# Attention: the weights for v taken from the sums' exponentials by fp32 transposes, instead of from transposed logits

## The chip, the cores and the metric

One NeuronCore of a Trainium2 chip runs the whole program; the other cores are idle. The metric is the device time of one execution in microseconds. The engines meant below are PE (TensorE: matrix products; PEld is its loading of weights), DVE (VectorE), ACT (ScalarE), POOL (GpSimd) and SP, whose queue issues the DMAs. PE's result goes to PSUM, which has room for 8 tiles of 128 x 512 fp32; DVE and ACT read it there.

## The reference

Two pre-norm residual layers over x (1 x 1024 x 1024, fp32) and a final RMSNorm. Layer 0 is a gated linear recurrence; layer 1 is attention with 16 heads of 64 and a forget gate, which is where the change lies:

```python
def fox_mixer(h, w_in, b_f, w_out):
    u = h @ w_in                                  # q, k, v, gate: 1024 each; f: 16
    ...
    cum = jnp.cumsum(jax.nn.log_sigmoid(f_logit), axis=1)
    # for each block of 128 queries:
        logits = jnp.einsum("bqhd,bkhd->bhqk", q_blk, kf) * scale
        logits = logits + (cq_blk[..., :, None] - ck[:, :, None, :])
        logits = jnp.where(mask, logits, NEG_INF)          # causal
        p = jax.nn.softmax(logits, axis=-1)
        o = jnp.einsum("bhqk,bkhd->bqhd", p, vf)
    y = o * jax.nn.silu(gate)
    return y @ w_out
```

The kernel's result has to stay close to fp32, so each product of two matrices is made of rounded halves: a value is split into hi (fp32r) and lo (the rest), and three products (hi hi, hi lo, lo hi) are added.

## The kernel before

The program has three stages. The first layer runs to about 430 us; then come its output projection, the norm and the first projections of layer 1 (to about 500 us); then the heads of attention, one after the other, to about 1120 us, with the output projection behind the last of them. This change concerns the heads.

For each head, q and k are projected for a pair of heads at a time (`kq_units`), split into hi and lo, and brought by DMA (`load`, L563) into two operand tiles: T (keys) and U (queries), 128 partitions x 2 x 1024, one of each for even and for odd heads. Their rows hold the halves and the forget gate's cumulative sums, so that two products give a logit with its gate term. A head has two halves c of 512 queries, and two functions work on each:

- `maxima(hd, c)` (L635): for each of four blocks of 128 queries, two products give the logits S with queries on partitions and keys along the row (L658, L659). DVE adds the causal mask and takes the maximum (L663); ACT takes the exponential in place and its sum (L666), of which only the sum is used. A transpose `mrow` (L672) and a product on DVE (L673) then write the negated maxima into four rows of U, so that the next function's logits come out with the maximum subtracted.
- `weigh(hd, c)` (L705): for pairs j of key blocks, two products (L727, L728) give the logits ST again, transposed: keys on partitions, queries along the row. ACT takes the exponential p (L733, L736), POOL sets the upper triangle of the diagonal block to zero (L741), DVE splits p into ph (L81, in `to_hi`) and pl (L86, in `to_lo`), and PE multiplies them with v into O (L761, L762).

An fp32r product in this stage is never narrower than 256 columns: S is widened by

```python
hi_ = max(hi_, lo_ + 256)          # L657
q0 = min(max(begin, j * P), end - 256)          # L723, ST and thereby O
```

S and ST share two PSUM slots of two banks each (tag "S"). While one half is weighed, the maxima of the next half are taken: `run(order, weigh, maxima, fill)` (L790) steps through a string, in which 0 is a step of the first function, 1 of the second, and "." a step of `fill`, the projections for later heads or, from head 13 on, the output projection (`partial`). `ORDERS` (L28) holds these strings. The framework's scheduler may then shift instructions within each engine's order by its own estimates.

Tiles of tag xp (three buffers) hold the finished heads' results y on their way back from DRAM (`load_y`, L809) and the residual stream in `partial` (L822).

## Time and profile before

| | us |
|---|---|
| median of 3 runs | 1159.39 (1158.55 to 1160.67) |
| the profiled execution | 1157.61 |
| its span (first to last instruction) | 1155.8 |
| PE busy | 1129.7 |
| DVE busy | 828.2 |
| ACT busy | 596.3 |
| POOL busy | 336.3 |

The profile is of one execution. In its rows "L727 PE MATMUL ST<-U,T" is line 727 of the kernel, on PE, a product that writes tile ST from U and T; behind the bar stand the group's busy time, the mean of one in ns, and the idle time of the engine just ahead of it, with what ended that. A fp32 product leaves two records (two passes), a transpose one. Durations of PE records overlap, since products are pipelined.

### The profile page before, as it was taken

What the parts mean: (1) busy time and instruction counts of PE and PEld (TensorE: products, weight loads), DVE (VectorE), ACT (ScalarE), POOL (GpSimd) and SP (SyncE); (2) the same over time, 40 slices, a digit from 0 to 9 for tenths busy, and PEclk for the clock granted to TensorE, in tenths of its full rate; (3) what the DMA queues carried; (4) which work ended last, traced back from release to release, by engine and by line L of the source; (5) the groups of instructions that cost most, each with busy time, mean ns of one, the idle gap of its engine ahead of it and who ended that gap; (6) DMA issues with size and microseconds to landing.
All of it is one profiled execution on the core that took longest, in us unless ns stands there. A gap on an engine that the chain in (4) does not pass through costs nothing.

```text
span 1155.8 us, 15813 instructions
## 1 busy us (share of the span) xinstructions
PE 1129.7 (98%) x5653; PEld 946.9 (82%) x5653; DVE 828.2 (72%) x1311; ACT 596.3 (52%) x1010; POOL 336.3 (29%) x328
## 2 busy tenths in 40 slices
PE   9999999999999999999999999999999999999995
PEld 7788888888888887978888988889888898777795
DVE  7589766677566889556877757777577776577776
ACT  8388345345544656454554545545455454445343
POOL 1212202112021103342333333323333334141445
PEclk9999999999999999999999999999999999999998
DMA  6111111111111124351343323433234331646544
GB/s 211 51 41 50 51 51 55 42 50 41 51 59 38 55 72 151 100 142 38 92 120 92 92 65 92 120 91 85 65 92 110 85 90 60 181 132 178 162 129 146
DMA packets 62701, 104.89 MB, mean 91 GB/s; under 512 B 8792, under 2 KB 27864, under 8 KB 62624
## 3 DMA queue, kind: packets, MB, share of 16 engines
q1 hardware_dynamic: 62624, 103.90, 32.1%
q8 instruction: 44, 0.72, 0.3%
q14 instruction: 33, 0.27, 0.1%
HBM read 62.78 MB, written 15.93 MB: 68 GB/s over the span
## 4 chain that ended last, share of the span: by engine, by line
PE 46%; DVE 6%; ACT 2%; DMA 2%; issue 1%; POOL 1%; DVEq 0%; ACTq 0%; SPq 0%; POOLq 0%
PE gps L111 6%; PE gps L113 6%; PE gps L112 6%; PE ST L727 3%; PE O L762 3%; PE S L659 2%; PE ST L728 2%; PE S L658 2%; PE O L761 2%; PE vps L523 2%; PE vps L521 2%; PE vps L522 2%; PE ops L111 2%; PE ops L113 2%; PE ops L112 2%
## 5 line engine op out<-in xcount | busy, mean ns | idle before, releaser
L86 POOL TENSOR_TENSOR wl<-wf,wh 128x512 fp32r<-128x512 f32 (+2 forms) x130 | 190.1, 1467 | 499.5 <-ACT wh L75 424.2
L111 PE MATMUL gps<-hh,wh 128*128 128x512 f32 x576 | 226.6, 394 | 0.5 <-DVE qkl L559 0.5
L113 PE MATMUL gps<-hl,wh 128*128 128x512 f32 x576 | 226.9, 394 | 0.0
L112 PE MATMUL gps<-hh,wl 128*128 128x512 f32 x576 | 226.6, 393 | 0.1
L75 ACT CAST wh<-wf 128x512 fp32r<-128x512 f32 (+2 forms) x156 | 94.0, 607 | 137.8 <-PE gps L113 43.3
L666 ACT ACTIVATE S<-S,st 128x128 f32<-128x128 f32 (+7 forms) x128 | 91.4, 714 | 114.1 <-DVE st L663 113.1
L113 PEld LDWEIGHTS gps<-hl,wh 128*128 128x128 f32 x576 | 108.3, 188 | 24.3
L112 PEld LDWEIGHTS gps<-hh,wl 128*128 128x128 f32 x576 | 108.5, 188 | 21.9 <-POOL wl L86 0.6
L111 PEld LDWEIGHTS gps<-hh,wh 128*128 128x128 f32 x576 | 108.4, 188 | 21.8 <-DVE qkl L559 0.9
L81 DVE CAST ph<-p 128x512 fp32r<-128x512 f32 (+2 forms) x130 | 80.0, 625 | 57.2 <-ACT p L733 30.1
L86 DVE TENSOR_TENSOR pl<-p,ph 128x512 fp32r<-128x512 f32 (+2 forms) x130 | 118.3, 927 | 2.4
L741 POOL TENSOR_SCALAR_AFFINE_SELECT p<-p 128x128 f32<-128x128 f32 (+1 forms) x128 | 49.1, 400 | 194.0 <-ACT p L736 95.0
L663 DVE CUSTOM_DVE_ANT_0 S<-S,mask 128x128 f32<-128x128 f32 (+7 forms) x128 | 96.6, 758 | 5.1 <-PE S L659 4.1
L355 DVE TENSOR_TENSOR x<-x,ops 128x512 f32<-128x512 f32 x80 | 54.0, 681 | 51.0 <-PE ops L113 50.9
L111 PE MATMUL ups<-hh,wh 128*128 128x512 f32 x192 | 76.1, 396 | 3.1 <-DVE us L265 1.9
L113 PE MATMUL ups<-hl,wh 128*128 128x512 f32 x192 | 76.0, 396 | 0.2
L112 PE MATMUL ups<-hh,wl 128*128 128x512 f32 x192 | 75.5, 393 | 0.0
L733 ACT ACTIVATE p<-ST 128x512 f32<-128x512 f32 (+1 forms) x68 | 53.0, 786 | 40.7 <-PE ST L728 37.6
L521 PE MATMUL vps<-wh,hh 128*128 128x256 f32 (+1 forms) x256 | 72.7, 285 | 0.0
L523 PE MATMUL vps<-wl,hh 128*128 128x256 f32 (+1 forms) x256 | 72.5, 285 | 0.2 <-POOL wl L86 0.2
L522 PE MATMUL vps<-wh,hl 128*128 128x256 f32 (+1 forms) x256 | 72.6, 284 | 0.0
L727 PE MATMUL ST<-U,T 128*128 128x512 f32 (+1 forms) x198 | 67.8, 350 | 2.3 <-ACT S L666 2.2
(192 smaller groups left out, 2580.9 us busy)
## 6 DMA issues: line engine op xcount, KB each, us to landing
wf<-in_w SPq DMA_DIRECT2D x100, 256.0 KB
wf<-in_wo SPq DMA_DIRECT2D x64, 128.0 KB
T<-qkh SPq DMA_DIRECT2D x28, 256.0 KB
U<-qkh SPq DMA_DIRECT2D x28, 256.0 KB
x<-in_xt SPq DMA_DIRECT2D x16, 256.0 KB
x1d<-x SPq DMA_DIRECT2D x16, 256.0 KB
wf<-in_wv SPq DMA_DIRECT2D x16, 256.0 KB
xp<-x1d SPq DMA_DIRECT2D x16, 256.0 KB
```

The costliest lines, as they stand in the source:

```text
L75: nc.scalar.copy(hi, src)
L81: eng.tensor_copy(hi, src)
L86: return eng.tensor_tensor(lo, src, f32(hi), ALU.subtract)
L111: nc.tensor.matmul(o, wh, xh[:, cs], start=i == 0, stop=False)
L112: nc.tensor.matmul(o, wl, xh[:, cs], start=False, stop=False)
L113: nc.tensor.matmul(o, wh, xl[:, cs], start=False, stop=i == len(pairs) - 1)
L521: nc.tensor.matmul(pt, xh, wh, start=k == 0, stop=False)
L522: nc.tensor.matmul(pt, xl, wh, start=False, stop=False)
L523: nc.tensor.matmul(pt, xh, wl, start=False, stop=k == KT - 1)
L663: nc.vector.tensor_tensor_reduce(S[:, :n], S[:, :n], mask[:, SEQ - n :], -1.0, -NEG, ALU.add, ALU.min, accum_out=m)
L666: seen[0] = nc.scalar.activation(S[:, :n], S[:, :n], AF.Exp, bias=f32(m), scale=-1.0, accum_out=sums[:, i : i + 1])
L727: nc.tensor.matmul(A[:, jj, :n], T[s][:, 0, ks], U[s][:, 0, q0:end], start=True, stop=False)
```

## The change

The exponentials that ACT takes for the sums are kept, in fp32 tiles p0 to p7 in SBUF, one for each block of 128 queries. They already have the maximum subtracted and the mask in them. `weigh` no longer computes logits: for each key block it turns the 128 x 128 blocks of p with PE transposes (fp32, against the identity) into a PSUM tile pt; ACT copies pt to ph, DVE subtracts to pl, and the products with v follow. The transposed logits, their exponentials, the selects on POOL, the maxima's transpose and the product on DVE are gone. A diagonal block now has its true width, so that the last key block of each half gives a product of 128 columns.

U is now three tiles of half the length: the first halves of even and odd heads share one (U0, tag "U"), and `load_q` loads each half by itself. The place of the copies to ph and pl in the buffers changes (three of 512 columns instead of two of 2 x 512). xp has two buffers instead of three, and the residual stream in `partial` uses two of another tag ("R"). The forget gate's scratch tiles move to other tags, and the steps in `ORDERS` are fewer, since the maxima have one step less.

```diff
-ORDERS = (("1.10111.0.10.", "1.1010.1.0.1..10"), (".1101.1..00..11.", "111.0.0.0.11.01...."))
+ORDERS = (("1.1011..0.10.", "1.1010.1.0....0"), (".1101.1..00..1.", "111.0.0.0.1.0...."))
...
-        U = [tu.tile([P, 2, SEQ], F32R, tag=f"U{s}", name=f"U{s}") for s in range(2)]
+        U0 = tu.tile([P, 2, HALF], F32R, tag="U", name="U")
+        U = [(U0, tu.tile([P, 2, HALF], F32R, tag=f"U{s}", name=f"U{s}")) for s in range(2)]
...
+        def load_q(hd, c):
+            s = hd % 2
+            u = U[s][c]
+            hi, lo = (f32(z[s * HD : (s + 1) * HD, halves[c]]) for z in kq[hd // 2, 0])
+            nc.sync.dma_start(f32(u[:64, 0]), hi)
+            nc.sync.dma_start(f32(u[64:, 0]), hi)
+            nc.sync.dma_start(f32(u[:64, 1]), lo)
+            nc.sync.dma_start(f32(u[64:66, 1]), cumd[hd, :, halves[c]])
...
+                p = ps_[i] = at.tile([P, n], F32, tag=f"p{i}", name="p", bufs=1)
                 seen[0] = nc.scalar.activation(
-                    S[:, :n], S[:, :n], AF.Exp, bias=f32(m), scale=-1.0, accum_out=sums[:, i : i + 1]
+                    p, S[:, :n], AF.Exp, bias=m, scale=-1.0, accum_out=sums[:, i : i + 1]
                 )
                 yield
-            pt = ps.tile([P, P], F32, tag="O", name="mrow")
-            nc.tensor.transpose(pt[:4], f32(st[:, 4 * c : 4 * c + 4]), ident)
-            nc.vector.tensor_tensor(
-                U[s][96:100, 1, c * HALF : (c + 1) * HALF].rearrange("p (a b) -> p a b", a=4),
-                pt[:4].unsqueeze(1).to_broadcast([4, 4, P]),
-                own,
-                ALU.mult,
-            )
-            yield
...
             for j0 in range(0, nj, 2):
-                A = ps.tile([P, 2, HALF], F32, tag="S", name="ST")
...
+                A = ps.tile([P, 2, HALF], F32, tag="S", name="pt")
+                qlo = [max(begin, j * P) for j in (j0, j0 + 1)]
+                ns = [end - q for q in qlo]
                 for jj in range(2):
-                    j = j0 + jj
-                    q0 = min(max(begin, j * P), end - 256)
...
-                    nc.tensor.matmul(A[:, jj, :n], T[s][:, 0, ks], U[s][:, 0, q0:end], start=True, stop=False)
-                    last[0] = nc.tensor.matmul(
-                        A[:, jj, :n], T[s][:, 1, ks], U[s][:, 1, q0:end], start=False, stop=True
-                    )
...
+                    ks = slice((j0 + jj) * P, (j0 + jj + 1) * P)
+                    for q in range(qlo[jj], end, P):
+                        o = q - qlo[jj]
+                        last[0] = nc.tensor.transpose(A[:, jj, o : o + P], ps_[q // P][:, ks], ident)
+                parts = []
                 for jj in range(2):
-                    ...
-                        nc.gpsimd.affine_select(
...
+                    a = A[:, jj, : ns[jj]]
+                    ph, pl = (at.tile([P, HALF], F32R, tag=t, name=t, bufs=3)[:, : ns[jj]] for t in ("ph", "pl"))
+                    to_hi(ph, a, nc.scalar)
+                    to_lo(pl, a, ph, nc.vector)
+                    parts.append((ph, pl))
+                for jj, (ph, pl) in enumerate(parts):
...
-                y = at.tile([P, HALF], F32, tag="xp", name="y", bufs=3)
+                y = at.tile([P, HALF], F32, tag="xp", name="y", bufs=2)
...
-                x = at.tile([P, HALF], F32, tag="xp", name="xp", bufs=3)
+                x = rpool.tile([P, HALF], F32, tag="R", name="xp")
```

PE's order at the end of head 1's second half, before. ST are head 1's transposed logits, S head 2's logits for the sums, O the products with v (one name of v for each key block):

```order
L762 MATMUL O<-pl,v_3792 128x512
L727 MATMUL ST<-U_3606,T_3604 128x512
L728 MATMUL ST<-U_3606,T_3604 128x512
L727 MATMUL ST<-U_3606,T_3604 128x384
L728 MATMUL ST<-U_3606,T_3604 128x384
L672 MATMUL mrow<-ident,st 4x128
L761 MATMUL O<-ph,v_3824 128x512
L727 MATMUL ST<-U_3606,T_3604 128x256
L728 MATMUL ST<-U_3606,T_3604 128x256
L727 MATMUL ST<-U_3606,T_3604 128x256
L728 MATMUL ST<-U_3606,T_3604 128x256
L762 MATMUL O<-pl,v_3824 128x512
```

The same place in the new order (pt are the transposed blocks of p):

```order
L653 MATMUL S<-T_3598,U 128x512
L654 MATMUL S<-T_3598,U 128x512
L722 MATMUL O<-ph,v_3818 128x512
L723 MATMUL O<-pl,v_3818 128x512
L722 MATMUL O<-ph,v_3850 128x512
L723 MATMUL O<-pl,v_3850 128x512
L710 MATMUL pt<-ident,p 128x128 x10
L722 MATMUL O<-ph,v_3913 128x512
L723 MATMUL O<-pl,v_3913 128x512
L722 MATMUL O<-ph,v_3945 128x384
L723 MATMUL O<-pl,v_3945 128x384
L722 MATMUL O<-ph,v_3977 128x256
```

Eight products with ST and one transpose of the maxima have become ten transposes, and the product with v of the key block just turned follows them at once, where before the products with v that stood there were those of an earlier key block.

ACT's order between a first and a second half of a head, before (p is the exponential of ST, S that for the sums):

```order
L733 ACTIVATE p<-ST 128x1024
L666 ACTIVATE S,sums<-S,st 128x512
L736 ACTIVATE p<-ST 128x512
L736 ACTIVATE p<-ST 128x384
L733 ACTIVATE p<-ST 128x2x256
L666 ACTIVATE S,sums<-S,st 128x640
```

And in the new order:

```order
L75 CAST ph<-pt 128x256
L75 CAST ph<-pt 128x128
L663 ACTIVATE p,sums<-S,m 128x640
L727 COPY yo<-O 64x512
L663 ACTIVATE p,sums<-S,m 128x768
L75 CAST ph<-pt 128x512
L75 CAST qkh<-gps_4875 128x512
L75 CAST ph<-pt 128x384
L663 ACTIVATE p,sums<-S,m 128x896
```

Where a second exponential stood, ACT now makes the copy to ph, one for each key block; the exponential for the sums now writes p.

More of the change, by code (lines that the diff above doesn't have):

```diff
@@ L591, in trunk @@
         cum = at.tile([HEADS, SEQ], F32, tag="sg", name="cum")
-        parts = [at.tile([HEADS, SEQ], F32R, tag=t, name="cp") for t in ("ph", "pl")]
         def forget(half):
@@ L598, in forget @@
                 nc.tensor.transpose(pt[:HEADS, i * P : (i + 1) * P], fz[:, half * 4 + i], ident)
-            z_, e_, hi, lo = z[:, cs], e[:, cs], *(c[:, cs] for c in parts)
+            z_, e_ = (at.tile([HEADS, HALF], F32, tag=t, name=n, bufs=3) for t, n in (("ph", "z"), ("pl", "e")))
+            parts = [at.tile([HEADS, HALF], F32R, tag=f"p{i + 2 * half}", name="cp", bufs=1) for i in (3, 4)]
+            hi, lo = parts
             nc.scalar.activation(z_, pt[:HEADS], AF.Identity, bias=bft)
@@ L610, in forget @@
             for i in range(2):
-                nc.sync.dma_start(cumd[:, i, cs], f32(parts[i][:, cs]))
+                nc.sync.dma_start(cumd[:, i, cs], f32(parts[i]))
             for hd in range(2):
                 if half == 0:
-                    load(hd, cs)
+                    load(hd, cs, (0,) if hd == 0 else ())
         first = values(0)
@@ L835, in final @@
             else:
-                xs = tu.tile([P, 4, 2, 256], F32, tag=("T0", "U0")[q], name="x1")
-                xs = [xs[:, d] for d in range(4)]
+                xs = [tu.tile([P, 4, 2, 256], F32, tag="T0", name="x1")] if q == 0 else []
+                xs += [tu.tile([P, 2, 2, 256], F32, tag=t, name="x1") for t in ("U", "U0")[: 2 * q]]
+                xs = [x[:, d] for x in xs for d in range(x.shape[1])]
             split = 3 if (c, q) == (1, 1) else 2
@@ L854, in final @@
                     lambda: (at if d else rpool).tile(
-                        [P, 2, 256], F32, tag="xp" if d else "R", name="sq1", bufs=3 if d else 2
+                        [P, 2, 256], F32, tag="xp" if d else "R", name="sq1", bufs=2
                     ),
@@ L909, in trunk @@
             next(fill)
-        load(0, slice(HALF, SEQ))
-        load(1, slice(HALF, SEQ))
-        run("00.0.00", maxima(0, 0), fill=fill)
+        load(0, halves[1], (1,))
+        load(1, halves[1], (1,))
+        run("00.0.0", maxima(0, 0), fill=fill)
+        load_q(1, 0)
         drain(fill)
```

87 lines of the change are left out of this document (22 added, 65 removed).

## The prediction

> **What bounds the kernel now.** I read the page first: busy time by engine, and the clock.
>
> ```profile
> span 1155.8 us, 15813 instructions
> PE 1129.7 (98%) x5653; PEld 946.9 (82%) x5653; DVE 828.2 (72%) x1311; ACT 596.3 (52%) x1010; POOL 336.3 (29%) x328
> PEclk9999999999999999999999999999999999999998
> PE 46%; DVE 6%; ACT 2%; DMA 2%; issue 1%; POOL 1%; DVEq 0%; ACTq 0%; SPq 0%; POOLq 0%
> ```
>
> TensorE (PE) is busy for 98% of the span at full clock, and no DMA or queue holds more than 2% of the chain that ended last. Next the stretches of the attention stage (from 500 us on), with a stretch of the first layer (the numbers in brackets count instructions), then PE's own waits (total, times, longest).
>
> ```profile
> core 0: us, PE busy (x) PEld busy (x) DVE busy (x) ACT busy (x) POOL busy (x), PEclk, DMA share, GB/s
> 60.00:430.00 370.00, 370.00 (x1602) 300.69 (x1601) 269.40 (x283) 201.27 (x236) 65.64 (x38) 1.00 0.17 50
> 500.00:1000.00 500.00, 496.92 (x2638) 426.04 (x2637) 355.26 (x667) 249.85 (x507) 173.27 (x187) 1.00 0.37 92
> 1000.00:1050.00 50.00, 47.11 (x220) 38.14 (x219) 33.64 (x60) 23.82 (x48) 16.95 (x19) 1.00 0.59 167
> 1050.00:1100.00 50.00, 48.46 (x231) 38.87 (x230) 39.54 (x71) 22.55 (x47) 16.43 (x21) 1.00 0.52 159
> ```
>
> ```profile
> PE O L762 <- DVE pl L86: 3.3, 4, 1.0
> PE ST L727 <- ACT S L666: 2.2, 3, 1.5
> PE O L761 <- DVE ph L81: 0.6, 1, 0.6
> PE ops L112 <- POOL wl L86: 0.7, 1, 0.7
> ```
>
> Between 500 and 1100 us PE stands still for only 3.1 + 2.9 + 1.5 = 7.5 us. So the time of this stage is the sum of what PE is fed, and work taken off DVE, ACT or POOL gives at most the waits: the three at the changed instructions (O and ST) are 3.3 + 2.2 + 0.6 = 6.1 us. The question is what PE loses and gains.
>
> **The price of a PE instruction.** The mean durations of the groups (some 0.39 us for 512 columns) are latencies of a pipeline and overlap; what counts is the distance from one to the next.
>
> ```profile
> 639.84 0.28 PE L521 MATMUL vps<-wh,hh 128*128 128x256 f32 x1
> 640.66 0.28 PE L522 MATMUL vps<-wh,hl 128*128 128x256 f32 x1
> L672 PE MATMUL mrow<-ident,st x32: 270/271/275, 517.6 to 1091.6; 128*4 128x128 f32 x32
> 479.74 0.38 PE L598 MATMUL fps<-ident,fz 128*16 128x128 f32 x2
> L137 PEld LDWEIGHTS sscol<-onesf,sq x80: 186/192/193, 443.6 to 1143.9; 128*128 128x128 f32 x80
> 1122.72 0.98 PEld L137 LDWEIGHTS sscol<-onesf,sq 128*128 128x128 f32 x8
> 0.00:3.00 3.00, 1.87 (x9) 1.87 (x9) 1.00 0.34 85
> 4.00:5.00 1.00, 1.00 (x9) 0.94 (x7) 1.00 0.76 175
> ```
>
> 512 columns: the stretch 60 to 430 holds almost only these, 370 / 1602 = 0.231 us. 256 columns: the first two rows are the first and the last of eight in a row, 0.82 / 7 = 0.117. 384 lies half way, 0.174. An fp32 transpose with 128 moving columns: two of them take 0.38 where one takes 0.271, so the second follows after 0.109. Those here load only 4 to 16 columns of weights; the new ones load 128. Loading 128 fp32 columns eight times in a row takes 0.98 where one load takes 0.19: 0.79 / 7 = 0.113 apart. And the last two rows are the ten fp32 products of 128 x 128 at the start (L64, two records each): 9 records in 1 us once they run fast, 0.111 each, load and stream together. A new transpose therefore costs 0.112, by the load rather than the stream.
>
> **The sum on PE.** Removed and changed groups:
>
> ```profile
> L727 PE MATMUL ST<-U,T 128*128 128x512 f32 x91 | 37.3, 410 | 1.9 <-ACT S L666 1.8
> L727 PE MATMUL ST<-U,T 128*128 128x256 f32 x76 | 20.1, 284 | 0.4 <-ACT S L666 0.4
> L727 PE MATMUL ST<-U,T 128*128 128x384 f32 x31 | 10.4, 336 | 0.0
> L761 PE MATMUL O<-ph,v 128*128 128x256 f32 x76 | 21.2, 284 | 0.6 <-DVE ph L81 0.6
> L145 PE MATMUL rsrow<-rs,onesf 128*128 128x512 f32 x8 | 4.1, 592 | 0.0
> 474.23 1.02 PE L145 MATMUL rsrow<-rs,onesf 128*128 128x512 f32 x2
> ```
>
> - The transposed logits go (L727, and L728 with the same counts): 182 x 0.231 + 62 x 0.174 + 152 x 0.117 = 42.0 + 10.8 + 17.8 = 70.6 us. The 32 transposes of the maxima (L672) go: 3.5. Together -74.1.
> - 576 transposes come (36 blocks of the lower triangle for each of 16 heads): 576 x 0.112 = +64.5. Bounds: 62.8 at 0.109, 65.1 at 0.113.
> - Of the 76 pairs of value products with 256 columns (L761, and L762 alike), 33 pairs now have 128, the block on the diagonal: 66 products. No row shows an fp32r product under 256 columns. The lower bound is the pace of weight loads, 0.112 instead of 0.117: -0.3. The upper is fp32's pace: rsrow's two passes over 512 columns lie 1.02 - 0.59 = 0.43 apart, 0.84 ns a column, against 0.45 for fp32r; at 128 columns that is two passes of 0.111 (the row from 4 to 5 us), 0.222 a product, 66 x 0.105 = +6.9. I take the upper end, because the nearest rows in width, 128 columns of four bytes, have that pace, and every fp32r product of this kernel is widened to 256 columns, at twice the streamed work for a 128-column block. Both ends stay in the range.
>
> Sum: -74.1 + 64.5 + 6.9 = -2.7 us.
>
> **Off PE.** The copies and selects:
>
> ```profile
> L81 DVE CAST ph<-p 128x512 fp32r<-128x512 f32 (+2 forms) x130 | 80.0, 625 | 57.2 <-ACT p L733 30.1
> L673 DVE TENSOR_TENSOR U<-mrow,own 4x512 fp32r<-4x512 f32 x32 | 21.9, 684 | 16.2 <-PE mrow L672 15.6
> L733 ACT ACTIVATE p<-ST 128x512 f32<-128x512 f32 (+1 forms) x68 | 53.0, 786 | 40.7 <-PE ST L728 37.6
> L736 ACT ACTIVATE p<-ST 128x512 f32<-128x512 f32 x31 | 18.5, 596 | 21.2 <-PE ST L728 20.0 <-DVE pl L86 1.2
> L736 ACT ACTIVATE p<-ST 128x384 f32<-128x384 f32 x31 | 15.1, 487 | 0.0
> L75 ACT CAST qkh<-gps 128x512 fp32r<-128x512 f32 x14 | 8.2, 587 | 18.2 <-DVE gps L498 17.9
> ```
>
> DVE loses 80.0 + 21.9 = 102 us. ACT loses its second exponentials (53.0, and 33.6 in L736's two forms) and gains 198 copies out of PSUM, 0.587 at 512 columns, less at the others: about 93 for 87, +6 us, at 50% busy. POOL loses its selects. All of this lies under PE's stream and I cost it at nothing; if DVE's relief emptied the three waits above, it would be worth up to 6.1.
>
> What else moves is also put at nothing. The query halves are loaded in 128 issues for 72; SP's share of the chain is 0%, and the half tile U that both head parities now share is asked for again only one half head later. Three buffers become two for y (and two of another tag serve xp). There the trace has a wait in SP's queue, behind which weight loads stand:
>
> ```profile
> SPq L823 <- DMA x1d<-xp: 20.8, 10, 3.1
> ACT yhh L75 <- DMA y<-y1d: 8.5, 4, 4.3
> ```
>
> PE met none of it but the 0.7 us at ops L112. If a weight load came late once for the longest of these, it would cost 3 to 4 us between 1000 and 1100.
>
> **The new waits.** A value product now needs its transposes, a copy on ACT and a subtraction on DVE; before, an exponential, (on the diagonal) a select, a copy and a subtraction. But the order also puts it nearer: at the end of head 1's second half ten transposes stand directly ahead of it. The same place before shows what such nearness costs:
>
> ```profile
> 577.71 0.28 PE L728 MATMUL ST<-U,T 128*128 128x256 f32 x1
> 578.76 0.50 PE L762 MATMUL O<-pl,v 128*128 128x512 f32 x1 [0.77 <-DVE pl L86]
> L86 DVE TENSOR_TENSOR qkl<-gps,qkh 128x512 fp32r<-128x512 f32 x16 | 11.0, 688 | 5.9 <-ACT qkh L75 5.9
> L666 ACT ACTIVATE S<-S,st 128x1024 f32<-128x1024 f32 x16 | 17.4, 1088 | 13.9 <-DVE st L663 13.8
> ```
>
> There four ST products go straight ahead of the product with pl, and PE idles 0.77 us. PE runs in order, so all that stands behind waits with it. In the new order the first copy (0.587) can run while the last six of the ten transposes do (6 x 0.112 = 0.67), and the subtraction after it (0.69 from PSUM) is covered only by one product of 0.231: about half a microsecond of wait, some more for the next pair. The first transposes of a half need the exponential of its last block (1.09); the first transposed logits needed the maxima's transpose and U's product (0.27 + 0.68), so they come 0.1 us later, and PE has projections to run there. Old and new waits are of one size, so I let them cancel, between -6.1 (they go) and +12 (rival 2).
>
> **Against the clock.** The profiled execution took 1157.6 us (span 1155.8, the rest around it), and -2.7 makes 1154.9. The median of the runs is 1159.4, 1.8 above it, so the forecast is 1159.4 - 2.7 = 1156.7 us, 0.23% faster. What this measurement can tell from no change is about 0.2%, 2.3 us: faster means under 1157.1, slower over 1161.7.
>
> **A rule of the Trainium skill.** The mrow row says 271 ns for one transpose, but the pair at 479.74 us shows the next one 0.109 behind. The Trainium skill, "TensorE: Matmul & The Clock Gate", Part 4, gives about 275 ns for a transpose in a kernel's context; as a latency the trace agrees (271), and as a price it would make 576 x 0.275 = 158 us and a forecast of some 1251, which the pair speaks against. The same section says that transposes do not count as activity for the clock gate; that is rival 4.
>
> **The rivals.**
> 1. The 128-column products run at the pace of their weight loads: -74.1 + 64.5 - 0.3 = -9.9, 1149.5 us. For it: fp32r's spacing falls evenly from 512 to 256 columns. Against it: the fp32 rows at 128.
> 2. Slower: the value products wait behind the transposes. Place: the rows with ten transposes directly ahead, and the diagonal pairs. Price 0.77 a wait, as measured at 578.76. Four waits more than now cancel the gain, seven (5.4 us) bring it past 1161.7, with the old ones unchanged; eight give 1156.7 + 6.2 = 1162.9, one in each of 16 second halves 1169. For it: the shorter distance in the order. Against it: DVE's 102 us less, and waits as large as these in the same place now.
> 3. The load of 128 columns isn't hidden behind the stream: 0.109 + 0.112 = 0.221 a transpose, +62.8, 1219 us. The 0.111 at the start speaks against it.
> 4. The clock drops where transposes stand together. The start shows the slow pace: 9 records in 1.87 us, 0.208, against 0.111. For the transposes alone this is 576 x 0.097 = +56, 1213 us. Against it: bursts are at most ten, 1.1 us, and the clock stayed 1.00 through the idle 2.9 us of 1000 to 1050.
> 5. The waits at O and ST go altogether, since DVE is free: 1156.7 - 6.1 = 1150.6.
>
> **Chances.** Forecast as summed, waits even (within 3 us): 0.45. Rival 1: 0.22; rival 2: 0.17; rival 3: 0.05; rival 4: 0.03; rival 5: 0.08. The range 1146 to 1165 takes in rival 1 with some waits gone and rival 2 up to ten waits, and leaves out rivals 3 and 4 and the ends of the others, about 0.18. The likeliest case's own range is 1153.5 to 1160. Faster: half of the forecast's 0.45 (its centre lies at the border), rivals 1 and 5: 0.53. Same: 0.19 of the forecast's, and a quarter of rival 2: 0.23. Slower: the rest of both, rivals 3 and 4: 0.24.
>
> **What the profile after would show.** The transposes x576 about 0.112 apart in their bursts, or near 0.22 (rival 3), and the granted clock below 1.00 in some stretch (rival 4). The 66 narrow value products followed after 0.22 or after 0.11. PE's waits at O near 4 us, with the transposes waiting for p instead of ST for S. DVE's busy time near 720. PE busy about 3 us less than 1129.7. The forecast is wrong if the narrow products are cheap, or if PE's waits between 500 and 1100 us change by more than 3 us.

## The result, and the profile after

The changed kernel takes 1166.9 us (median of 6 runs, 1163.8 to 1168.2) against 1159.5 for the kernel before beside it: ratio 1.0056, 95% interval 1.0041 to 1.0070. It is slower by 7.5 us where 1156.7 was forecast. Executions of one kernel differ along with their mean granted clock: of the changed kernel's six, the one at 0.995 took 1163.8 us and the one at 0.990 took 1167.8. From the page of the changed kernel, the span, the engines, the clock and the chain:

```profile
span 1165.0 us, 16009 instructions
PE 1129.6 (97%) x5801; PEld 945.1 (81%) x5801; DVE 721.1 (62%) x1219; ACT 603.5 (52%) x1078; POOL 269.2 (23%) x198
PEclk9999999999999999999999999999999999999998
PE 85%; DVE 5%; DMA 5%; POOL 2%; ACT 1%; issue 1%; SPq 1%; DVEq 0%; POOLq 0%; ACTq 0%
```

DVE lost 107 us of work, the clock is as before, and PE's busy time is the same to 0.1 us. The span is longer by 9.2 us. The stretches of the attention stage, with the columns of the prediction, show where PE stands still:

```profile
500.00:1000.00 500.00, 487.25 (x2714) 413.78 (x2713) 263.69 (x575) 249.20 (x546) 119.46 (x82) 1.00 0.35 89
1000.00:1050.00 50.00, 46.24 (x228) 37.74 (x227) 27.67 (x55) 24.34 (x52) 10.65 (x9) 1.00 0.62 178
1050.00:1100.00 50.00, 48.40 (x248) 40.39 (x247) 29.46 (x64) 25.80 (x57) 13.05 (x11) 1.00 0.49 158
```

PE is idle for 12.8 us in the first of these, where it was 3.1; in the other two 3.8 and 1.6, close to the 2.9 and 1.5 before. PE's waits in this stage by what ended them (total, times, longest):

```profile
PE O L723 <- DVE pl L86: 7.6, 20, 1.0
PE O L722 <- ACT ph L75: 3.2, 9, 0.4
PE ops L111 <- DVE sg L629: 2.5, 1, 2.5
PE vps L519 <- POOL wl L86: 2.0, 3, 1.1
PE S L653 <- ACT p L663: 1.2, 1, 1.2
```

The value products with pl wait 20 times, with ph 9 times. Below them stand three waits that took 0.7 us or less before. The transposes themselves go as forecast: this row gives shortest, median and longest record, and where one transpose follows another their ends lie 0.109 apart (median of 453).

```profile
L710 PE MATMUL pt<-ident,p x576: 270/272/329, 525.4 to 1126.5; 128*128 128x128 f32 x192
```

Idle time tells less than the loss here. A product that has waited shows as 0.51 us where its like show 0.40, so a part of each wait counts as busy. I therefore measured each PE instruction between 500 and 1100 us from the end of the one before to its own end, took off the spacing of its width (0.231 us for 512 columns, 0.175 for 384, 0.117 for 256, 0.112 for 128), and added up what was over 0.06. This sum, called lateness below, is 12.1 us before and 32.9 after: O 6.1, then 23.8; ST 4.4, then gone with its products; v's projection (vps) none, then 2.8; the output projection (ops) 0.9, then 2.8; S none, then 2.6. The granted clock is 1.00 throughout this stage in both traces.

One of the places, the second half of head 1, by start and duration, from the timeline (rows of the other engines' other work are left out):

```profile
576.99 0.59 ACT L75 CAST ph<-pt 128x512 fp32r<-128x512 f32 x1 [1.18 <-PE pt L710]
577.61 0.69 DVE L86 TENSOR_TENSOR pl<-pt,ph 128x512 fp32r<-128x512 f32 x1 [1.54 <-ACT ph L75]
...
578.34 0.58 ACT L75 CAST ph<-pt 128x512 fp32r<-128x512 f32 x1 [0.76 <-DVE pl L86]
...
578.80 0.70 DVE L658 CUSTOM_DVE_ANT_0 S<-S,mask 128x512 f32<-128x512 f32 x1 [0.50 <-PE S L654]
...
579.42 0.69 DVE L86 TENSOR_TENSOR pl<-pt,ph 128x512 fp32r<-128x512 f32 x1
...
580.16 0.51 PE L723 MATMUL O<-pl,v 128*128 128x512 f32 x1 [0.69 <-DVE pl L86]
...
580.51 1.25 PE L710 MATMUL pt<-ident,p 128*128 128x128 f32 x10
581.52 0.58 ACT L75 CAST ph<-pt 128x512 fp32r<-128x512 f32 x1 [1.15 <-PE pt L710]
```

The second copy on ACT waits for DVE's subtraction of the first block, though the two blocks lie in different halves of pt: the built program lets ACT and DVE read one PSUM tile only in turn (with a tile for each block, in run 3, this wait is gone). So the chain of a pair is copy, subtraction, copy, subtraction, 0.59 + 0.69 + 0.58 + 0.69 us and the changes of engine. And DVE took a maximum of S ahead of the second subtraction, 0.5 us more; PE waits for it, with the next ten transposes behind. The same two engines as totals (for what, us, times, longest):

```profile
DVE pl L86 <- ACT ph L75: 105.6, 84, 4.2
ACT ph L75 <- DVE pl L86: 39.8, 60, 1.2
```

### The profile page after: what moved, and what is told of

Read it like the earlier page. It is cut to its first block, busy times and chain, and to the rows that moved or that the text cites. A ratio compares the mean times of both kernels' runs of the same rounds, so it can differ in the third digit from the quotient of the medians.

```text
span 1165.0 us, 16009 instructions
## 1 busy us (share of the span) xinstructions
PE 1129.6 (97%) x5801; PEld 945.1 (81%) x5801; DVE 721.1 (62%) x1219; ACT 603.5 (52%) x1078; POOL 269.2 (23%) x198
## 4 chain that ended last, share of the span: by engine, by line
PE 85%; DVE 5%; DMA 5%; POOL 2%; ACT 1%; issue 1%; SPq 1%; DVEq 0%; POOLq 0%; ACTq 0%
PE gps L111 10%; PE gps L112 10%; PE gps L113 10%; PE ops L111 5%; PE ops L113 5%; PE ops L112 5%; PE pt L710 4%; PE ups L113 4%; PE ups L111 4%; PE ups L112 4%; PE S L653 3%; PE O L723 3%; PE S L654 3%; PE vps L519 2%; PE O L722 2%; PE vps L518 2%
## 5 line engine op out<-in xcount | busy, mean ns | idle before, releaser
L86 POOL TENSOR_TENSOR wl<-wf,wh 128x512 fp32r<-128x512 f32 (+2 forms) x130 | 183.0, 1411 | 690.7 <-ACT wh L75 587.2
L111 PE MATMUL gps<-hh,wh 128*128 128x512 f32 x576 | 230.0, 400 | 0.4 <-DVE qkl L555 0.4
L86 DVE TENSOR_TENSOR pl<-pt,ph 128x512 fp32r<-128x512 f32 (+1 forms) x198 | 106.0, 539 | 119.2 <-ACT ph L75 105.6
L75 ACT CAST ph<-pt 128x512 fp32r<-128x512 f32 (+1 forms) x198 | 91.9, 468 | 140.4 <-PE pt L710 88.5
L663 ACT ACTIVATE p<-S,m 128x128 f32<-128x128 f32 (+7 forms) x128 | 94.9, 742 | 77.2 <-DVE m L658 76.8
L113 PEld LDWEIGHTS gps<-hl,wh 128*128 128x128 f32 x576 | 108.4, 188 | 23.6
L710 PE MATMUL pt<-ident,p 128*128 128x128 f32 x576 | 82.9, 272 | 0.0
L723 PE MATMUL O<-pl,v 128*128 128x512 f32 (+1 forms) x198 | 71.1, 364 | 8.6 <-DVE pl L86 7.6
L710 PEld LDWEIGHTS pt<-ident,p 128*128 128x128 f32 x576 | 69.0, 140 | 9.9 <-ACT p L663 0.4
L722 PE MATMUL O<-ph,v 128*128 128x512 f32 (+1 forms) x198 | 69.8, 354 | 3.3 <-ACT ph L75 3.2
```

What stands on the lines that cost most here:

```text
L75: nc.scalar.copy(hi, src)
L86: return eng.tensor_tensor(lo, src, f32(hi), ALU.subtract)
L111: nc.tensor.matmul(o, wh, xh[:, cs], start=i == 0, stop=False)
L113: nc.tensor.matmul(o, wh, xl[:, cs], start=False, stop=i == len(pairs) - 1)
L663: seen[0] = nc.scalar.activation(p, S[:, :n], AF.Exp, bias=m, scale=-1.0, accum_out=sums[:, i : i + 1])
L710: last[0] = nc.tensor.transpose(A[:, jj, o : o + P], ps_[q // P][:, ks], ident)
```

## The experiments

My first theory was this chain: it ends too late for the products behind it. The rivals were VectorE's load, the two PSUM slots shared with S, the strings of the order, the buffers, and the price of the instructions. Ratios are to the kernel before, run beside each, whose medians were 1159.4 to 1160.3; they differ from the quotient of the two medians by up to 0.12%. Runs 1, 5, 6 and 17 leave the low halves of the weights out of the result: they are for taking the time apart and are no complete kernels.

**1. Without the subtraction.**

```diff
-                    to_lo(pl, a, ph, nc.vector)
-                    parts.append((ph, pl))
+                    parts.append((ph, ph))
```

> The changed kernel without the subtraction to pl: the second value product of each key block reads ph again, so the low halves of the weights are left out. TensorE is fed exactly the same. Theory (the gain of some 15 us on TensorE is eaten by value products that wait for a chain copy, subtraction, copy, subtraction of about 2.6 us behind the last transpose, in which the second copy waits for the first subtraction): the time falls by 10 to 16 us from the changed kernel's 1166.9, to 1151-1157, and the waits at the value products with pl, 18-20 us, go almost entirely. Rival 'elsewhere' (the time went to the loads of U, the two xp buffers, the late weights on GpSimd, the logits' slots): at most -4 us, 1163 or more. Rival 'price of transposes' (they cost more than their spacing shows): no change.

1144.6 us, ratio 0.9866 (0.9845 to 0.9886): 22 us less than the changed kernel, more than the 10 to 16 expected. PE is fed as much as there, and its stretch from 500 to 1000 us is nearly full:

```profile
500.00:1000.00 500.00, 497.47 (x2815) 431.24 (x2814) 199.74 (x441) 259.33 (x568) 122.41 (x85) 1.00 0.38 97
```

The lateness is 8.6 us. So with few waits the rewrite is worth some 15 us, and the miss lies in waits, not in PE's work. It doesn't yet say by which way the subtraction makes them.

**2. Value products one pair later.**

```diff
+                    if held:
+                        products(*held.pop(0))
+                held = parts
```

> The changed kernel with the value products of a pair of key blocks emitted one pair later, between the copies of the next pair; the work is the same. Theory (distance between transposes and value products): the chain of 2.6 us is covered by the next pair's transposes, 0.9 us, and by what stands between, so the waits at the value products fall from about 24 us of excess to 8-14 and the time to 1152-1158. Rival 'engines' (ScalarE and VectorE can't deliver faster, wherever the products stand) and rival 'elsewhere': within 3 us of 1166.9. The scheduler may move the products back: then the rows of the order near the ends of heads 1, 5 and 9 wait as before.

1164.9 us, ratio 1.0047 (1.0029 to 1.0064). The prediction of my theory failed. O's lateness fell from 23.8 to 15.5 us, but the transposes' and S's rose to 5.9 and 6.9 (total 29.5). PE's waits in its trace:

```profile
PE pt L718 <- DVE pl L86: 4.2, 9, 0.8
PE O L707 <- DVE pl L86: 3.4, 12, 0.5
PE S L653 <- ACT p L663: 3.3, 2, 1.7
PE O L706 <- ACT ph L75: 2.6, 9, 0.4
```

The transposes now wait for the subtraction, because it holds the PSUM slot. What is gained at O is given back at the slot.

**3. A PSUM tile for each key block.**

```diff
-                A = ps.tile([P, 2, HALF], F32, tag="S", name="pt")
+                A = [ps.tile([P, HALF], F32, tag="S", name="pt") for _ in range(2)]
```

> The changed kernel with a PSUM tile of its own for each key block's transposed weights, where a pair shared one: the second copy on ScalarE then no longer waits for VectorE's subtraction of the first block, nor the first copy for the second block's transposes. The pair now takes both slots that it shares with the logits S. Theory (serial chain): the chain shortens from copy, subtraction, copy, subtraction (2.6 us behind the last transpose) to about copy, subtraction, subtraction less the overlap with transposes (1.5 us), worth 4 to 9 us where the slots allow it: 1158-1163. Rival 'slots': logits and transposes now queue for slots, TensorE's waits at S and pt grow by more than the chain gives, 1168-1180. Rival 'elsewhere': 1165-1168.

1188.0 us, ratio 1.0240 (1.0213 to 1.0267). The second copy no longer waits for the first subtraction in the built program, but the pair takes both slots, and the rival named 'slots' came, and stronger than I had put it:

```profile
PE pt L710 <- ACT p L663: 13.0, 17, 2.3
PE O L722 <- ACT ph L75: 11.1, 23, 0.8
```

The transposes wait 17 times, by this row for an exponential. The run can't price the shorter chain, since it changes both.

**4. The copies on VectorE.**

```diff
-                    to_hi(ph, a, nc.scalar)
+                    to_hi(ph, a, nc.vector)
```

> The changed kernel with the copies to ph on VectorE instead of ScalarE: about 92 us move from ScalarE's busy time to VectorE's (721 to some 815). The chain copy, subtraction, copy, subtraction is as long as before, on one engine, without the changes of engine (about 0.1 us each). Theory (length of the chain): 1164-1169, little change, since the chain keeps its length. Rival 'ScalarE is too busy' (the copies queue behind the exponentials of the logits): the time falls by 5 us or more, to 1162 or less. Rival 'VectorE is too busy' (it would be the engine that delivers late): 1171 or more.

1186.6 us, ratio 1.0225 (1.0197 to 1.0253). I had expected little change; the rival of a VectorE too busy, 1171 or more, came. DVE's busy time is 809.5, below the 828 of the kernel before, and yet

```profile
PE O L723 <- DVE pl L86: 15.6, 25, 1.6
PE vps L519 <- POOL wl L86: 4.3, 4, 1.8
```

So the products come later with the copies in VectorE's queue, at 69% busy: the share of busy time said nothing of it. Part of it is the chain itself, since a copy of 512 columns takes 0.69 us there and 0.59 on ScalarE.

**5 and 6. The subtraction aside, and in place but unread.** In both, both value products read ph.

```diff
-                    to_lo(pl, a, ph, nc.vector)
+                    to_lo(pl, f32(ph), ph, nc.vector)      # aside: from SBUF, nobody waits
```

> As the run without the subtraction (1144.6), but VectorE does 198 subtractions again, aside: from ph in SBUF to a tile that nobody reads; both value products read ph, so the low halves are left out. VectorE's busy time is back near 720 (or some 20 less, if the subtraction is faster from SBUF), while neither the second copy nor a product nor the PSUM slot waits for it. Theory 'chain' (the wait for the subtraction is what costs the 22 us): 1144-1149. Rival 'VectorE's load' (it was the 96 us less work on VectorE, by which the logits' maxima came earlier): 1158-1167.

> The changed kernel with the subtraction in its place, from PSUM to pl, so that the second copy and the PSUM slot wait for it as before; but both value products read ph, so the low halves are left out and no product waits for pl. Theory 'products' (the cost lies in TensorE's direct wait for pl): near the run without the subtraction, 1145-1150. Theory 'slot' (the long hold of the two slots shared with the logits is what costs; with the products put later the waits moved to the transposes and the logits): 1155-1165. The distance between this run, the one aside and the changed kernel divides the 22 us into the two.

Aside: 1155.8 us, ratio 0.9962 (0.9949 to 0.9975), between the two expectations, so both missed. Unread: 1161.7, ratio 1.0015 (0.9999 to 1.0031), as 'slot' had it. Read as a ladder this gives 11 us for VectorE's time, 6 for holding the slot, 5 for the products' wait. The traces forbid the first step. PE's order in the run aside is nearly that of run 1 (aligned by output tile and shape, 48 of 3,566 rows from 500 us on stand elsewhere), and its waits are

```profile
PE pt L710 <- ACT p L663: 7.8, 4, 2.4
PE vps L519 <- POOL wl L86: 3.6, 4, 1.6
```

The lateness at three transposes, 2.57 us each at 580.4, 727.3 and 873.4 us, is 7.7 of the 14.2 us by which this trace's lateness exceeds run 1's. Another 3.9 lie in three stretches of 3.4 us in which the granted clock is 0.50; two of these begin 1.3 to 1.5 us after the first two of the transposes. The first of the three transposes in the timeline:

```profile
575.39 3.48 DVE L86 TENSOR_TENSOR pl<-ph 128x512 fp32r<-128x512 f32 x2 [0.39 <-ACT ph L75]
...
575.55 2.77 POOL L690 TENSOR_TENSOR sg<-sg,recb 64x1024 f32<-64x1024 f32 x1 [5.89 <-DMA recb<-recd]
...
578.79 0.69 DVE L658 CUSTOM_DVE_ANT_0 S<-S,mask 128x512 f32<-128x512 f32 x1
...
579.58 0.69 ACT L663 ACTIVATE p<-S,m 128x512 f32<-128x512 f32 x1 [3.73 <-DVE m L658]
...
580.41 0.55 PE L710 MATMUL pt<-ident,p 128*128 128x128 f32 x3 [2.35 <-ACT p L663]
```

Two subtractions that take 0.69 each elsewhere took 3.48 us beside GpSimd's product, now that both their inputs are in SBUF. The Trainium skill, "GPSIMD Engine Reference", "1. Specifications", says that GpSimd and VectorE share SBUF interfaces and contend where a VectorE instruction has two SBUF inputs; the trace agrees. A cost came in that the changed kernel hasn't: its longest subtraction, from PSUM, is 0.693. What the rows do show is the loop: the maximum of S stands behind the subtractions in VectorE's queue, the exponential behind the maximum, the next transposes behind the exponential. One late subtraction comes back to PE as a late transpose.

Of unread, PE's waits are

```profile
PE O L722 <- ACT ph L75: 6.5, 18, 0.5
PE S L653 <- DVE pl L86: 3.3, 8, 0.9
```

No product waits for pl, but the logits wait for the slot that the subtraction holds. PE's order moved against the changed kernel too (250 of 3,564 rows), so the steps of 6 and 5 us are differences of orders too.

**7. Both copies first, then both subtractions.**

```diff
                     to_hi(ph, a, nc.scalar)
-                    to_lo(pl, a, ph, nc.vector)
                     parts.append((ph, pl))
+                for jj, (ph, pl) in enumerate(parts):
+                    to_lo(pl, A[:, jj, : ns[jj]], ph, nc.vector)
```

> The changed kernel with both copies of a pair ahead of both subtractions. The first subtraction now waits for the second copy, so the chain is copy, copy, subtraction, subtraction: as long in sum, with one change of engine for three. Theory 'the changes of engine cost' (each lets other work of the queue go ahead): 1157-1163. Theory 'length only': 1165-1170, since the first product with pl comes 0.6 us later and the products with ph of the second block earlier.

1171.3 us, ratio 1.0092 (1.0078 to 1.0106), at the upper end of 'length only' or a little over it. Fewer changes of engine didn't help. Nor is this a price of the chain alone: O's lateness fell to 14.5 us, that of v's projection rose to 10.6.

**8. The kernel before with narrow value products alone.**

```diff
-                    o = O[:, qlo[jj] - begin :]
-                    nc.tensor.matmul(o, v, ph[:, jj, : ns[jj]], start=j == 0, stop=False)
+                    w = max(begin, j * P) - qlo[jj]
+                    o = O[:, qlo[jj] + w - begin :]
+                    nc.tensor.matmul(o, v, ph[:, jj, w : ns[jj]], start=j == 0, stop=False)
```

> The kernel before with one part of the change alone: the 66 value products on the second diagonal block have 128 columns for 256 (logits, exponentials and copies stay 256 wide). By the spacing of 60 ns in the changed kernel's trace against 117: 66 x 0.057 = 3.8 us less, 1155-1156.5. By the prediction's upper end (0.222 a product): 1166. By its lower end: 1159.

1155.4 us, ratio 0.9957 (0.9944 to 0.9970): 5.0 us less, within 3.5 to 6.5. It is the fastest complete kernel of the study, ahead of both the kernel before and the changed one. Its PE rows at one diagonal pair:

```profile
557.71 0.28 PE L762 MATMUL O<-ph,v 128*128 128x256 f32 x1
557.83 0.28 PE L763 MATMUL O<-pl,v 128*128 128x256 f32 x1
557.95 0.22 PE L762 MATMUL O<-ph,v 128*128 128x128 f32 x1
558.01 0.28 PE L763 MATMUL O<-pl,v 128*128 128x128 f32 x1
```

Start and duration give the ends: 558.11, 558.17, 558.29. The first narrow product ends 0.06 behind a wide one, the second 0.12 behind the narrow one. Over all 33 pairs it is 0.061 and 0.112. My expectation had put 0.060 on both; two wide value products take 2 x 0.118, so the sum of the spacings is 33 x (0.236 - 0.173) = 2.1 us less, and lateness fell by 1.0; together 3.1, a little under the interval. The rest may be the clock: the five executions have a median granted clock of 0.994, those of the kernel before beside them 0.992.

**9, 10 and 13. Other strings for the odd heads.** The fill of heads 1, 5 and 9 has eight steps, and each dot takes one. The change's strings use five in the first half, three early in the second; the last four dots find nothing.

```diff
-("1.1011..0.10.", "1.1010.1.0....0")       # the change's
+("1.1011..010.", "1.101.01.0.0")           # run 9: four and four
+("1.10110.10.", "1.10.1.01.0.0")           # run 10: three and five
+("1.10111.0.10.", "1.1010.1.0.1..10")      # run 13: those of before
```

> The changed kernel with another string for odd heads: 1.1011..010. and 1.101.01.0.0 for 1.1011..0.10. and 1.1010.1.0....0. In heads 1, 5 and 9 the fill has only 8 steps; the changed strings spend 5 of them in the first half and 3 early in the second, and the last four dots of the second find no fill, so its last pairs of key blocks stand with nothing between. Now 4 and 4, with fill between the second half's later steps. Theory 'fill': the three clusters of 4.5 to 5.5 us of waits (569 to 584, 719 to 734, 868 to 883 us) shrink by half, so 5 to 8 us less, 1159-1162. Rival 'latency everywhere' (the chain is late wherever the fill stands): the waits move to the first halves, 1165-1168.

> As the run before, with three of the eight fill steps in the first half of an odd head and five in the second: 1.10110.10. and 1.10.1.01.0.0. Theory 'fill': as good or better than four and four if the second half, with four pairs against two, needs more cover: 1157-1162. Rival: the first half then waits instead, 1162-1168.

> The changed kernel with the odd heads' strings of the kernel before, 1.10111.0.10. and 1.1010.1.0.1..10 (the surplus steps of the maxima do nothing). Four of the eight fill steps then stand in the first half, as before the change, for five. Theory 'strings' (the edit of the strings turned a bearable chain into waits): 1158-1162, near the second string's 1159.2. Theory 'distance' (only fill between the later steps helps, and the old strings put the fill early in the second half too): 1164-1168, near the first string's 1165.9.

Four and four: 1165.9 us, ratio 1.0048 (1.0031 to 1.0066), where my theory had 1159 to 1162. Three and five: 1159.2, ratio 0.9990 (0.9978 to 1.0001). Those of before: 1160.7, ratio 0.9999 (0.9986 to 1.0012). Undoing the edit of the strings, and nothing else, thus takes back 0.57% by the ratios, 6.6 us (6.2 by the medians). O's lateness: 23.8 with the change's strings, 23.6, 11.8, 14.5. In the trace of three and five the wait for pl is down to

```profile
PE O L723 <- DVE pl L86: 3.1, 11, 0.5
```

The clusters at 569 to 584, 719 to 734 and 868 to 883 us, 4.0 us in seven waits at O each, shrank to 1.4 us in four. Where the fill stands decides, not only how much there is: 9 differs from 13 in few characters and brought nothing.

**11. The kernel before with two xp buffers.**

```diff
-                y = at.tile([P, HALF], F32, tag="xp", name="y", bufs=3)
+                y = at.tile([P, HALF], F32, tag="xp", name="y", bufs=2)
-                x = at.tile([P, HALF], F32, tag="xp", name="xp", bufs=3)
+                x = rpool.tile([P, HALF], F32, tag="R", name="xp")
```

> The kernel before with one part of the change alone: the tiles of y have two buffers for three and the residual stream uses two of tag R. The changed kernel's trace shows 2.8 us at a product of the output projection (1020.74) and 1.5 at a logit (1029.03), where before had 0.7 in that stretch. If these waits come from the buffers: 1161-1163. If they come from the order of the attention steps around them: 1159-1160.

1163.0 us, ratio 1.0017 (1.0004 to 1.0031): slower by 2.0 us, within 0.5 to 3.6. This part of the change has a price of its own.

**12. The kernel before with all true widths.**

```diff
-                    q0 = min(max(begin, j * P), end - 256)
+                    q0 = max(begin, j * P)
-                    hi_ = max(hi_, lo_ + 256)
```

> The kernel before with every product at its true width: value products and transposed logits of the second diagonal block 128 columns for 256 (66 each, with their exponentials, splits and selects), the first block's logits 128 for 256 (32 products). 164 products x 0.057 = 9.3 us less on TensorE; with the value products alone it measured 4.9 less, 1155.4. Theory 'spacing' (a narrow fp32r product follows after 60 ns, and the rest of the time adds up): 1150-1152. Rival 'waits come back' (TensorE, faster there, waits for ScalarE and VectorE at the diagonal): 1153-1157.

1166.3 us, ratio 1.0054 (1.0035 to 1.0073): slower, with less PE work. A last pair of 256 and 128 columns no longer goes through ACT and DVE in one instruction:

```profile
PE 1132.1 (97%) x5653; PEld 946.5 (81%) x5653; DVE 827.7 (71%) x1377; ACT 594.5 (51%) x1043; POOL 325.3 (28%) x328
```

```profile
PE O L761 <- DVE pl L86: 4.8, 8, 0.9
PE O L760 <- DVE ph L81: 3.3, 1, 3.3
```

DVE has 66 instructions more, ACT 33, and the lateness is 22.1 for 12.1. The theory 'spacing', 1150 to 1152, fell; 'waits come back' holds, beyond its number.

**14, 15, 16 and 18. Towards a faster version.** 14 is run 10 with the first block's logits 128 wide (the line of `hi_` taken out); 15 adds a step of fill between two pairs in even heads; 16 is run 8 with the same narrow logits; 18 is run 14 with three xp buffers and two for pl.

```diff
-(".1101.1..00..1.", "111.0.0.0.1.0....")
+(".1101.1.0.0..1.", "111.0.0.0.1.0....")       # run 15
```

> The changed kernel with the second string (1159.2) and the first query block's logits 128 wide for 256: 32 products x 0.057 = 1.8 us less on TensorE, with no more instructions on VectorE or ScalarE (both work on the true width already). Theory 'spacing': 1157-1158. Rival 'waits come back': 1159-1161.

> As the run before, with .1101.1.0.0..1. for .1101.1..00..1. in even heads' first halves: a step of fill between the two pairs of key blocks that stood side by side. In the second string's trace eight products on the diagonal with 128 columns wait 0.53 each, 4.3 us together. If those are the pairs side by side: 2 to 4 us less than the run before, 1154-1156. If they sit elsewhere (odd heads): no change.

> The kernel before with value products 128 wide on the second diagonal block (1155.4) and the first query block's logits 128 wide for 256; the transposed logits, their exponentials and splits stay 256 wide, so that no instruction is added on ScalarE, VectorE or GpSimd. 32 x 0.057 = 1.8 us less: 1153-1154.5. If the slower run with all true widths (1166.3) came from the logits S and not from the split exponentials and casts of the last pair: 1157 or more.

> The changed kernel with the second string and the first block's logits 128 wide (1158.2), with three xp buffers again for y, the residual stream and the squares; to make room pl has two buffers for three. If the 2.4 us that two xp buffers cost in the kernel before are lost here too, and a third pl buffer isn't needed: 1155-1156.5. If pl's two buffers make the subtraction wait for products: 1159 or more.

14: 1158.2, ratio 0.9987 (0.9976 to 0.9998), near the 1157 to 1158 expected. 15: 1159.6, ratio 1.0008 (0.9994 to 1.0021). 16: 1157.1, ratio 0.9975 (0.9963 to 0.9986), where 1153 to 1154.5 was expected: narrow logits added to run 8 gained nothing. 18: 1165.3, ratio 1.0063 (1.0041 to 1.0085). In 15 the diagonal products with 128 columns wait as in 14, 4.8 us in 14 places, so 'no change' held; the transposes' lateness went from 0.7 to 4.9, of which 4.4 is one wait at 1015.6 us. In 18 that of S rose from 2.5 to 10.7, and the subtraction waits 28 times for a product, 38.8 us, where in 14 it was 8 times, 10.5: two buffers for pl cost more than a third for xp gave. None beats run 8.

**17. Without the subtraction, strings of before.**

> The changed kernel without the subtraction (the low halves of the weights left out; both value products read ph) and with the odd heads' strings of before. Without the subtraction the changed strings gave 1144.6. Theory 'strings act through the chain': the same within 2 us, 1143-1147, and the chain with the old strings costs 1160.7 - 1145 = 16 us. Rival 'strings act by themselves' (they also move the logits or the projections): 5 us or more less, 1139 or under.

1158.6 us, ratio 0.9986 (0.9973 to 0.9999). My theory expected 1143 to 1147 and fell. Without any subtraction, and with strings that with it were the better ones, the lateness is 26.0 us, at other places:

```profile
PE vps L519 <- POOL wl L86: 7.4, 4, 3.2
PE pt L710 <- ACT p L663: 4.3, 5, 0.9
```

So the 22 us of run 1 are no fixed price of the chain: with the strings of before, the subtraction costs 2.1 us (run 13 against this one). What it costs hangs on the order.

**The account over all runs.** Time = 1159.5 + change of PE's work + (lateness - 12.1). PE's work is -13.4 us for the changed kernel (-74.1 removed, 576 x 0.109 = +62.8, narrow products -2.1), 1.1 less with narrow logits, -2.1 in run 8, -3.2 in 16, -5.3 in 12, 0 in 11.

| run | lateness | by the account | measured |
|---|---|---|---|
| after | 32.9 | 1166.9 | 1166.9 |
| 1 without subtraction | 8.6 | 1142.6 | 1144.6 |
| 2 products later | 29.5 | 1163.5 | 1164.9 |
| 3 tile for each block | 47.5 | 1181.5 | 1188.0 |
| 4 copies on DVE | 47.7 | 1181.7 | 1186.6 |
| 5 aside | 22.8 | 1156.8 | 1155.8 |
| 6 unread | 29.7 | 1163.7 | 1161.7 |
| 7 copies first | 33.9 | 1167.9 | 1171.3 |
| 8 narrow, before | 11.1 | 1156.4 | 1155.4 |
| 9 four and four | 31.8 | 1165.8 | 1165.9 |
| 10 three and five | 22.2 | 1156.2 | 1159.2 |
| 11 two xp, before | 17.7 | 1165.1 | 1163.0 |
| 12 true widths, before | 22.1 | 1164.2 | 1166.3 |
| 13 old strings | 25.9 | 1159.9 | 1160.7 |
| 14 | 23.0 | 1155.9 | 1158.2 |
| 15 | 26.2 | 1159.1 | 1159.6 |
| 16 | 11.1 | 1155.3 | 1157.1 |
| 17 | 26.0 | 1160.0 | 1158.6 |
| 18 | 30.8 | 1163.7 | 1165.3 |

Except for 3 and 4 it holds within 3.4 us. That the first row closes to a tenth is luck: lateness comes from one profile of each, whose execution can lie some microseconds from the median (run 6: 1166.0 for 1161.7), and by the two profiled spans the account of the changed kernel is 1.8 us short. It is bookkeeping, too: it says that the time is PE's spacings plus what comes late, not why that comes late.

A part of lateness is the clock. In eight of the 20 traces, those of the two kernels among them, it is 1.00 from 500 to 1100 us. In the other twelve it is 0.50 in one to three stretches, of 3.4 or 6.8 us; 18 of these 20 stretches stand beside a wait of PE of over 2.1 us, and 18 of the 22 waits as long as that have one beside them. Products that wait for nothing lose 1.1 to 1.6 us in a stretch of 3.4 us; in run 17 this is 4.1 of the 26.0 us, in run 5 3.9 of 22.8. Where such a stretch stands, a long wait costs more than its own length; the changed kernel's profile has one wait as long, 2.8 us at 1020 us, and no stretch beside it.

## Why the prediction was wrong

- *What bounds the kernel*: right. PE's stream sets the time, and the loss is in what PE waits for.
- *Transposes at 0.112*: right, 0.109 measured, 62.8 for 64.5 us. Rival 3 (load not hidden) didn't occur, nor rival 4 (the clock) in the profile after, where the granted clock is 1.00 through the whole stage. Where it fell in other runs, it was beside long waits of PE.
- *Narrow products, upper end +6.9*: mis-sized by 9 us. They cost -2.1. The nearest rows in width were fp32's, and those go in two passes; I took the padding in the source as a hint, which it was not. Even the lower bound was too high, because the first narrow product follows the wide one ahead after 0.061 us: its load (from 557.83 us in run 8's trace) runs beside that product. The Trainium skill, "TensorE: Matmul & The Clock Gate", Part 2, "Back-to-back issue gap", gives about 81 ns sustained at 128 columns. The mean of the pairs here is 86, so for this width the trace agrees; for 512 columns it gives about 131, where the traces have 231. By its 81 an estimate of the term would have been 66 x (0.081 - 0.117) = -2.4.
- *"Old and new waits are of one size, so I let them cancel"*: this is the step that failed. Lateness went from 12.1 to 32.9 us, +20.8, beyond my bound of +12; PE's idle time between 500 and 1100 us alone went from 7.5 to 18.1, past the 3 us that I had named as a sign of being wrong. With the transposes' and the narrow products' terms put right, the sum is 1159.5 - 13.4 + 20.8 = 1166.9. Rival 2 named the mechanism and the place, head 1's second half, and its scale reached 1169; but I gave it 0.17 and ended the range at ten waits of 0.77 us. What was wrong is the count: it had one wait at each second half. In heads 1, 5 and 9 there are seven at O in a row, 0.28 to 0.96 us each, and at diagonal pairs two or three more.
- Two things in that step were wrong by reading. I let the first copy run beside the last transposes and the two blocks' copies and subtractions overlap; the program serves ACT and DVE in turn on one PSUM tile. Before, the split read p from SBUF, free of that. The rows at 576.99, which starts when the last of its transposes has ended, and at 578.34 with its 0.76 show it.
- *The edit of the strings* was described and not priced. It is worth some 6 us of the 7.5 by which the changed kernel is slower (run 13).
- *xp's two buffers at nothing*: 2.0 us in the kernel before (run 11), below the 3 to 4 I named, and not nothing.
- *DVE's relief is worth at most the old waits*: DVE's 720 came (721.1), the relief didn't: the waits at O rose from 3.9 to 10.8 us in the profile's rows. A busy share of 62% hid that a subtraction can stand behind other work in DVE's queue (the maximum at 578.80).
- *PE busy about 3 us less* as a sign of the narrow price: busy time can't tell it, since waiting products are longer records.

**What stays open.** Which link of the chain costs how much. Runs 6 and 17 changed PE's order along with the link (17 against 13: 710 of some 3,560 rows), and run 5 brought in a cost of its own. A version with every engine's order held fixed wasn't tried. Nor is it shown how much of the differences between executions the half-clock stretches make, since only one execution of each kernel was profiled.

## What to carry to other kernels

When a kernel is bound by one in-order engine, sum its work by end-to-end spacings, then ask of each moved step what stands directly behind it and what its whole chain takes, engine by engine, including who may read one PSUM tile at a time. The waits are a term of their own, here larger than the gain in work (20.8 against 13.4 us), and they follow the order: a string that looks like housekeeping was worth half of that gain. An experiment that takes one operation away under a scheduler can change the order too: compare where the waits stand, not only the times.

## What the runs showed of the hardware

A 128-column fp32r product with 128 columns of weights follows after 0.061 us behind a wide product and after 0.112 behind another narrow one (run 8, 33 pairs). fp32 transposes with 128 columns of weights go 0.109 apart in bursts of up to ten at a granted clock of 1.00, while each record shows 0.272; in the stretches of runs 14 and 15 with a granted clock of 0.50 (from 1012.5 and 1015.9 us) it is 0.21. A DVE subtraction of two SBUF operands, 0.69 us at 512 columns, took up to 2.88 while GpSimd multiplied two SBUF tiles (run 5); with one operand in PSUM none of the changed kernel's 198 was over 0.693. The kernel before, whose subtraction reads two SBUF tiles, had this too: 15 of its 130 took 1.65 to 3.37 us (the median at 1024 columns is 1.2), all of them beside GpSimd's work; the changed kernel is free of it.
